# A recurrent-layer encoder step on one core: norm of two column blocks laid out half a weight tile earlier, two blocks of branch tile 4 ordered before the gates of tile 0

## The chip, the cores and the metric

The kernel runs on one core of a Trainium2 chip. The metric is device time in microseconds (us) of one execution. The engines of the core are named as in the profile: PE (TensorE matmul), PEld (its weight load), DVE (VectorE), ACT (ScalarE), POOL (GpSimd) and SP (SyncE, which here only issues DMAs). Each engine works through its own queue in order; semaphores order one engine's work behind another's.

## The reference, cut to what matters

The reference is one inference step of a two-layer encoder over 1024 new frames of one stream and 32 more frames of a second one (1056 tokens, model width 1024). Layer A is a gated linear recurrence of width 1408, layer B is attention in a sliding window. Only the first half of layer A is touched by the change:

```python
u = rmsnorm(x, norm_pre) @ w_in                 # 1024 -> 2 x 1408
branch, gate = u[..., :D_RNN], u[..., D_RNN:]
conv = conv_b + ext[:, 0:T] * conv_w[0]         # ext: branch behind 3 older rows
for tap in range(1, CONV_W):                    # 4 taps along time
    conv = conv + ext[:, tap:tap + T] * conv_w[tap]
xb = conv.reshape(B, T, 16, 88)                 # blocks of 88 channels
r = sigmoid(einsum('btnc,ncd->btnd', xb, w_r) + b_r)
i = sigmoid(einsum('btnc,ncd->btnd', xb, w_i) + b_i)
...
y = (h * silu(gate)) @ w_out
return x + rmsnorm(y, norm_post), new_conv, new_h
```

Each channel is convolved along time with four taps; the recurrence gates r and i are products of the convolved channels with 16 small matrices of 88 x 88.

## The kernel before, in words

**Layout.** Channels lie on the 128 partitions, tokens along the free dimension. The 1408 recurrent channels are 11 tiles of 128 (`MR`), the 1024 input channels 8 (`KD`). The tokens are three column blocks (`NSA`): 0 to 384, 384 to 768, and 768 to 1060 (292 columns, with three columns of gap). A product for one tile and one column block fills one bank of PSUM; `bank` hands out eight of them in turn.

**Precision.** A float32 product is made of three reduced ones: every operand is split into a high part and a residual (`split`, lines 112 to 117: ACT rounds, VectorE or POOL subtracts; names with `hi`/`h` and `lo`/`l`). `mm3` (lines 146 to 152) issues three matmuls for each of the contraction tiles, on lines 150, 151 and 152: 24 for one column block of a branch tile.

**The norm.** The RMS norm of a token is a factor for a column, and is applied after the product. `x_stat(n)` takes the squares of the rows of column block n on ACT (line 281), makes the reciprocal roots on VectorE (283 to 286) and writes them on diagonals (`diag`, 289). `x_norm(n)` (lines 291 to 306) spreads them over all partitions with three small matmuls against ones (line 296, tile `rs`, held in their order by `pin`), copies the result to SBUF on ACT (299 to 302), then evacuates that column block of the first three branch tiles with it (line 207, VectorE), and convolves them (line 222 on ACT for tap 0, line 224 on VectorE for taps 1 to 3) and splits the result into `chi` and `clo` (116, 117).

**The first three tiles** go by column block: all three tiles for block 0, then for block 1, then for block 2 (`first_mm`, lines 310 to 313, and the loop at 328 to 335). `x_norm(0)` stands behind the second tile of block 1, `x_norm(1)` behind the first tile of block 2, `x_norm(2)` behind the loop.

**Tiles 3 to 10** go whole (loop at 445 to 464). In step t the kernel traces the three blocks of branch tile t with their evacuation, the weights of tile t + 2 (`prep_in`), the convolution, the gate weights of tile t - 1, then the gates of the tile that `GATES_AT[t]` names (tile 0 in step 3), the split of the convolution and the packing of tile t - 1, and the recurrence.

**Gates.** A gate of tile t needs its own convolution (lines 150 to 152, in the profile `gt<-chi` and `gt<-clo`) and some rows of the neighbouring tiles, since 88 does not divide 128. These rows are gathered by DMA into a `pack` tile (`pack_rows`, line 371: high parts issued from ACT, residuals from SP), which two more matmuls use (390, 391). Tile 0 needs 48 rows of tile 1. Tile 0 has thirty gate matmuls: two gates, three column blocks, five each.

**Weights.** `weights` loads a tile of weights in two halves on SP's queue (line 129, ring `raw` of four), and splits them into rings of six. For the tiles in `LO_POOL` (here 3, 4, 5 and gates 0 and 1) POOL makes the residual.

**The order of each engine's queue** is made by a planner that runs over the traced program: it takes what is ready by its own estimates, in the order of the program, with parts under `urgent` ahead by 300 places. `pin` ties an instruction behind the one traced before it on the same engine.

Of the kernel before, what the change touches and what calls it, by code (L numbers as in the profile page):

```python
# [63 lines left out]
def _trunk(ctx, tc, nc, A):  # L64
# [11 lines left out]
    def urgent(offset=300):  # L76
        return tc.high_priority(offset=offset)

    def pin(i, on=True):
        return tc.keep_in_program_order(i) if on else i  # L80

    def bank(name, tag="mm", bufs=None):
        return psum.tile([P, 512], F32, tag=tag, name=name, bufs=bufs or nbank)
# [28 lines left out]
    def split(dst_hi, dst_lo, src, lo_eng=None, hi_dve=False, behind=False):  # L112
        if hi_dve:
            V.tensor_copy(dst_hi, src)
        else:
            pin(S.activation(dst_hi, src, AF.Copy), behind)  # L116
        (lo_eng or V).tensor_tensor(dst_lo, src, dst_hi.bitcast(F32), op=ALU.subtract)  # L117
# [5 lines left out]
    def weights(src, kn, name, gain=None):  # L123

        out = []
        for k0 in range(0, kn, 4):
            kk = min(4, kn - k0)
            raw = ring.tile([P, 4, P], F32, tag="raw", bufs=4, name=f"raw_{name}_{k0}")
            nc.sync.dma_start(raw[:, :kk, :], src[:, k0:k0 + kk, :])
            if gain is not None and name not in GAIN_ACT:  # L130
                with urgent():
                    G.tensor_tensor(raw[:, :kk, :], raw[:, :kk, :],
                                    gains[:, gain * KD + k0:gain * KD + k0 + kk].unsqueeze(2).to_broadcast([P, kk, P]),
                                    op=ALU.mult)
            hi = ring.tile([P, 4, P], F32R, tag="whi", bufs=6, name=f"whi_{name}_{k0}")
            lo = ring.tile([P, 4, P], F32R, tag="wlo", bufs=6, name=f"wlo_{name}_{k0}")
            with urgent():
                if name in GAIN_ACT:
                    for i in range(kk):
                        split_scaled(hi[:, i, :], lo[:, i, :], raw[:, i, :], g_of(gain, k0 + i))  # L140
                else:
                    split(hi[:, :kk, :], lo[:, :kk, :], raw[:, :kk, :], G if name in LO_POOL else None, name in HI_DVE)
            out += [(hi[:, i, :], lo[:, i, :]) for i in range(kk)]
        return out

    def mm3(ps, ws, xs, last=True):

        n = len(ws)
        for i, ((wh, wl), (xh, xl)) in enumerate(zip(ws, xs)):
            nc.tensor.matmul(ps, wh, xh, start=i == 0, stop=False)  # L150
            nc.tensor.matmul(ps, wh, xl, start=False, stop=False)  # L151
            nc.tensor.matmul(ps, wl, xh, start=False, stop=last and i == n - 1)  # L152

# [24 lines left out]
    def row(name, dt=F32, w=W + 3):  # L178
        return rows.tile([P, W + 3], dt, tag="row", bufs=NROW, name=name)[:, :w]

    wts = {}

    def prep_in(m):
        wts[m] = weights(A["w_in_a"][m], KD, f"ina{m}")

    def x_of(c0, c1):
        return [(xhi[k][:, c0:c1], xlo[k][:, c0:c1]) for k in range(KD)]

    conv, chl, ext, gw, pack = {}, {}, {}, {}, {}

    def branch_mm(t, ns=(0, 1, 2)):
        if t not in ext:
            ext[t] = row(f"ext{t}")
            G.memset(ext[t][:, 0:3], 0.0)
        banks = []
        for n in ns:
            c0, c1 = NSA[n]
            ps = bank(f"br{t}_{n}")
            mm3(ps[:, :c1 - c0], wts[t], x_of(c0, c1))
            banks.append((n, ps))  # L200
        return banks

    def branch_evac(t, banks):
        for n, ps in banks:
            c0, c1 = NSA[n]
            with urgent():
                V.tensor_tensor(ext[t][:, 3 + c0:3 + c1], ps[:, :c1 - c0], rs[:, c0:c1], op=ALU.mult)

    def branch_conv(t, n=None):

        c0, c1 = (0, W) if n is None else NSA[n]
        e = ext[t]
        if c0 == 0:
            conv[t] = row(f"conv{t}", w=W)
            chl[t] = (row(f"chi{t}", F32R, W), row(f"clo{t}", F32R, W))
        if c1 == W:
            G.tensor_copy(convst[:, t, 0, :], e[:, SEQ:SEQ + 3])
            G.tensor_copy(convst[:, t, 1, :], e[:, S0 + DEC:S0 + DEC + 3])
            G.tensor_copy(e[:, S0:S0 + 3], pa[:, t, 9:12])
            del ext[t]  # L220
        c = conv[t][:, c0:c1]
        pin(S.activation(c, e[:, c0:c1], AF.Identity, bias=pa[:, t, 4:5], scale=pa[:, t, 0:1]), n == 0)  # L222
        for k in (1, 2, 3):
            V.scalar_tensor_tensor(c, e[:, c0 + k:c1 + k], pa[:, t, k:k + 1], c, op0=ALU.mult, op1=ALU.add)  # L224
        if n is not None:
            split(*(x[:, c0:c1] for x in chl[t]), c)
# [48 lines left out]
    def x_stat(n, rows_):  # L275

        s, y, m, r = (stat[:, i, 3 * n:3 * n + 3] for i in range(4))
        with urgent():
            for t, xr in zip(range(3 * n, 3 * n + 3), rows_):
                k = P if t < 8 else DEC  # L280
                pin(S.activation(xr[:k], xr[:k], AF.Square, accum_out=stat[:k, 0, t:t + 1]), t in (0, 3))
            S.activation(y, s, AF.Abs_reciprocal_sqrt, bias=epst, scale=1.0 / 1024.0)
            V.tensor_scalar(m, s, 1.0 / 1024.0, EPS, op0=ALU.mult, op1=ALU.add)
            V.tensor_tensor(m, m, y, op=ALU.mult)
            V.scalar_tensor_tensor(m, m, -0.5, y, op0=ALU.mult, op1=ALU.mult)
            V.scalar_tensor_tensor(r, m, 1.5, y, op0=ALU.add, op1=ALU.mult)
            for i, t in enumerate(range(3 * n, 3 * n + 3)):
                k = P if t < 8 else DEC
                V.tensor_scalar(diag[:k, t * P:t * P + k], ident[:k, :k], stat[:k, 3, t:t + 1], None, op0=ALU.mult)

    def x_norm(n):

        ps = bank(f"rs{n}")
        for i, t in enumerate(range(3 * n, 3 * n + 3)):
            m = P if t < 8 else DEC
            pin(nc.tensor.matmul(ps[:, i * P:i * P + m], ones[:m], diag[:m, t * P:t * P + m], start=True, stop=True))
        with urgent():
            if n < 2:
                S.activation(rs[:, NSA[n][0]:NSA[n][1]], ps[:, :384], AF.Copy, scale=1024.0)
            else:  # L300
                S.activation(rs[:, 768:SEQ], ps[:, :256], AF.Copy, scale=1024.0)
                S.activation(rs[:, S0:S0 + DEC], ps[:, 256:256 + DEC], AF.Copy, scale=1024.0)
        for m in range(NS):
            branch_evac(m, open_[n][m])
        for m in range(NS):
            branch_conv(m, n)

    open_ = {0: [], 1: [], 2: []}

    def first_mm(n, m):  # L310
        if n == 0 and m:
            prep_in(m)
        open_[n].append(branch_mm(m, (n,)))

    x_split(0)
    for m in range(NS):
# [10 lines left out]
    x_stat(1, xr[1])  # L327
    for n in (1, 2):
        for m in range(NS):
            first_mm(n, m)  # L330
            if m == 2 - n:
                x_norm(n - 1)
        if n == 1:
            x_stat(2, xr[2])
    x_norm(2)
# [26 lines left out]
    def prep_gate(t):  # L362
        gw[t] = weights(A["wg"][t], 4 + 2 * (NATIVE[t] is not None), f"gate{t}")

    def pack_rows(t):

        pk = row(f"pack{t}", F32R, W)
        h, off = sum(n for _, _, n in PACKED[t]), 0
        for s_, r0, n in PACKED[t]:
            for x in range(2):  # L370
                (nc.sync if x else nc.scalar).dma_start(pk[x * h + off:x * h + off + n, :].bitcast(F32),
                                                       chl[s_][x][r0:r0 + n, :].bitcast(F32))
            off += n
        pack[t] = (pk, 2 * h)
# [69 lines left out]
    GATES_AT = ((), (), (), (0,), (1,), (2,), (3,), (4,), (5,), (6,), (7,), (8, 9, 10))  # L444
    for t in range(MR):
        if t >= NS:
            branch_evac(t, branch_mm(t))
        wts.pop(t)
        if t >= NS - 2:
            prep_in(t + 2)  # L450
        with urgent():
            if t >= NS:
                branch_conv(t)
            if t >= 1:
                prep_gate(t - 1)
        ri = [gates(i) for i in GATES_AT[t]]
        with urgent():
            if t >= NS:

                split(*chl[t], conv[t], behind=True)  # L460
            if t >= 1:
                pack_rows(t - 1)
        for i, g in zip(GATES_AT[t], ri):
            recur(i, g)
# [183 lines left out]
    for n in (1, 2):  # L648
        last = orders[-1][:-1 - REUSE:-1]
        orders.append(last + [m for m in orders[-1] if m not in last])  # L650
    na = []
    for n, order in enumerate(orders):
        zs, acc = {}, []
        w = NSB[n][1] - NSB[n][0]
        for i, m in enumerate(order):
            if i + 1 < KD and f"{n}_{order[i + 1]}" not in wts:
                prep_outa(n, order[i + 1])
            ws = wts[f"{n}_{m}"]
            if n < 2 and i >= KD - REUSE:
                wts[f"{n + 1}_{m}"] = ws  # L660
            ps = bank(f"oa{m}_{n}")[:, :w]
# [579 lines left out]
```

## Time and profile before

| | |
|---|---|
| median of three runs | 914.59 us (914.43 to 915.57) |
| the profiled execution | 918.22 us, its span 916.4 us |
| TensorE busy | 891.0 us, 97% of the span |
| VectorE busy | 721.5 us, 79% |
| ACT busy | 562.8 us, 61% |
| POOL busy | 212.5 us, 23% |
| mean granted TensorE clock | 0.993 |

Times in the profile count from the start of the span. In a timeline a row is: start, duration, engine, line, operation, output <- inputs, shapes, how many of them, and in brackets how long the engine had been idle before it and which instruction released it. A matmul's duration covers its passage through the array, so the step from one start to the next is the time that it costs. In the view of windows a row is a stretch: its length, then busy time and number of instructions of PE, PEld, DVE, ACT and POOL, the granted TensorE clock as a share of full speed, the share of the DMA engines that is busy, and GB/s. The list of waits gives for each pair the total, the number and the longest.

### The profile page before, as it was taken

What the parts mean: (1) busy time and instruction counts of PE and PEld (TensorE: products, weight loads), DVE (VectorE), ACT (ScalarE), POOL (GpSimd) and SP (SyncE); (2) the same over time, 40 slices, a digit from 0 to 9 for tenths busy, and PEclk for the clock granted to TensorE, in tenths of its full rate; (3) what the DMA queues carried; (4) which work ended last, traced back from release to release, by engine and by line L of the source; (5) the groups of instructions that cost most, each with busy time, mean ns of one, the idle gap of its engine ahead of it and who ended that gap; (6) DMA issues with size and microseconds to landing.
All of it is one profiled execution on the core that took longest, in us unless ns stands there. A gap on an engine that the chain in (4) does not pass through costs nothing.

```text
span 916.4 us, 15897 instructions
## 1 busy us (share of the span) xinstructions
PE 891.0 (97%) x5434; PEld 864.6 (94%) x5434; DVE 721.5 (79%) x1571; ACT 562.8 (61%) x1231; POOL 212.5 (23%) x263
## 2 busy tenths in 40 slices
PE   9989999999999999999999999999999999899997
PEld 8989999999999999999989899999999998889985
DVE  5796878878897663185987758999989998898686
ACT  8747877869453334364663327666666766797661
POOL 5240222114300001124354521122212111202130
PEclk9989999999999999999999999999999999999999
DMA  9532433342543325445556586256347346424884
GB/s 336 197 84 67 134 94 118 93 123 88 174 134 118 89 83 163 133 145 183 161 173 191 167 235 155 95 158 184 96 131 212 95 118 183 136 96 137 288 268 160
DMA packets 95778, 137.35 MB, mean 150 GB/s; under 512 B 16145, under 2 KB 64305, under 8 KB 95697
## 3 DMA queue, kind: packets, MB, share of 16 engines
q1 hardware_dynamic: 86040, 123.30, 44.4%
q10 hardware_dynamic: 9480, 12.49, 4.4%
q8 instruction: 43, 0.70, 0.3%
q0 software_dynamic: 176, 0.54, 0.2%
q14 instruction: 39, 0.31, 0.1%
HBM read 99.28 MB, written 32.13 MB: 143 GB/s over the span
## 4 chain that ended last, share of the span: by engine, by line
PE 62%; DVE 19%; DMA 4%; ACT 3%; issue 3%; SPq 1%; POOL 1%; DVEq 0%; ACTq 0%; POOLq 0%
PE gb L151 5%; PE gb L152 5%; PE gb L150 5%; PE obm L698 4%; PE gB L698 4%; PE oa L151 4%; PE oa L150 4%; PE oa L152 4%; PE br L151 3%; PE br L150 3%; PE br L152 3%; PE ot L698 2%; DVE T L967 2%; DVE pl L117 2%; DVE P L927 2%
## 5 line engine op out<-in xcount | busy, mean ns | idle before, releaser
L150 PE MATMUL oa<-yh,whi_outa 128*128 128x384 f32 (+1 forms) x264 | 85.8, 325 | 0.0
L151 PE MATMUL gb<-xlo,whi_ina 128*128 128x384 f32 (+1 forms) x264 | 85.5, 324 | 0.0
L152 PE MATMUL gb<-xhi,wlo_ina 128*128 128x384 f32 (+1 forms) x264 | 85.3, 323 | 0.0
L150 PE MATMUL gb<-xhi,whi_ina 128*128 128x384 f32 (+1 forms) x264 | 85.1, 322 | 0.0
L151 PE MATMUL oa<-yl,whi_outa 128*128 128x384 f32 (+1 forms) x264 | 85.1, 323 | 0.0
L152 PE MATMUL oa<-yh,wlo_outa 128*128 128x384 f32 (+1 forms) x264 | 85.0, 323 | 0.0
L930 ACT ACTIVATE P<-P,sm 128x256 f32<-128x256 f32 (+1 forms) x132 | 64.0, 486 | 26.4 <-DVE sm L927 26.1
L150 PE MATMUL br<-xhi,whi_ina 128*128 128x384 f32 (+1 forms) x240 | 78.4, 327 | 0.0
L151 PE MATMUL br<-xlo,whi_ina 128*128 128x384 f32 (+1 forms) x240 | 78.4, 326 | 0.0
L152 PE MATMUL br<-xhi,wlo_ina 128*128 128x384 f32 (+1 forms) x240 | 77.8, 325 | 0.0
L117 DVE TENSOR_TENSOR wlo_outa<-raw_outa,whi_outa 128x512 fp32r<-128x512 f32 (+1 forms) x60 | 43.7, 741 | 42.0 <-ACT whi_outa L116 41.9
L616 POOL TENSOR_TENSOR qp<-qp,qp 128x384 f32<-128x384 f32 (+2 forms) x34 | 39.2, 1154 | 149.4 <-ACT qp L614 137.5
L698 PE MATMUL gB<-xh,whi_g 128*128 128x384 f32 (+1 forms) x192 | 63.2, 329 | 0.0
L698 PE MATMUL gB<-xh,wlo_g 128*128 128x384 f32 (+1 forms) x192 | 63.1, 329 | 0.0
L698 PE MATMUL gB<-xl,whi_g 128*128 128x384 f32 (+1 forms) x192 | 62.9, 328 | 0.0
L116 ACT ACTIVATE whi_outa<-raw_outa 128x512 fp32r<-128x512 f32 (+1 forms) x60 | 35.4, 594 | 41.9 <-PE oa L151 24.3
L224 DVE SCALAR_TENSOR_TENSOR conv<-ext,pa,conv 128x1060 f32<-128x1060 f32 (+2 forms) x51 | 50.1, 1005 | 9.0 <-ACT conv L222 8.6
L927 DVE CUSTOM_DVE_ANT_0 P<-S,mask,nsnk 128x256 f32<-128x256 f32 (+1 forms) x128 | 52.8, 461 | 0.1
L150 PEld LDWEIGHTS oa<-yh,whi_outa 128*128 128x128 f32 x264 | 49.6, 188 | 0.4
L151 PEld LDWEIGHTS oa<-yl,whi_outa 128*128 128x128 f32 x264 | 49.5, 188 | 0.4
L152 PEld LDWEIGHTS oa<-yh,wlo_outa 128*128 128x128 f32 x264 | 49.6, 188 | 0.0
L150 PEld LDWEIGHTS gb<-xhi,whi_ina 128*128 128x128 f32 x264 | 49.6, 188 | 0.0
(303 smaller groups left out, 2913.2 us busy)
## 6 DMA issues: line engine op xcount, KB each, us to landing
raw_ina<-w_in_a SPq DMA_DIRECT2D x44, 256.0 KB, 2.9
raw_outa<-w_out_a SPq DMA_DIRECT2D x40, 256.0 KB, 2.6
raw_ob<-w_out_b SPq DMA_DIRECT2D x32, 256.0 KB, 2.7
qscr<-quadq SPq DMA_DIRECT2D x8, 768.0 KB
Q<-qscr SPq DMA_DIRECT2D x32, 192.0 KB, 5.2
hscr<-u SPq DMA_DIRECT2D x11, 530.0 KB, 3.3
xr<-xr SPq DMA_DIRECT2D x8, 512.0 KB, 10.3
raw_g<-w_in_b SPq DMA_DIRECT2D x16, 256.0 KB, 2.6
```

What stands on the lines that cost most here:

```text
L116: pin(S.activation(dst_hi, src, AF.Copy), behind)
L117: (lo_eng or V).tensor_tensor(dst_lo, src, dst_hi.bitcast(F32), op=ALU.subtract)
L150: nc.tensor.matmul(ps, wh, xh, start=i == 0, stop=False)
L151: nc.tensor.matmul(ps, wh, xl, start=False, stop=False)
L152: nc.tensor.matmul(ps, wl, xh, start=False, stop=last and i == n - 1)
L224: V.scalar_tensor_tensor(c, e[:, c0 + k:c1 + k], pa[:, t, k:k + 1], c, op0=ALU.mult, op1=ALU.add)
L616: G.tensor_tensor(sums[0], sums[0], q, op=ALU.add)
L698: nc.tensor.matmul(ps, l, r, start=c == 0, stop=c == 3 * n - 1)
L927: V.tensor_tensor_reduce(pt[:, h, :w], sb[:, (h - h0) * 256:(h - h0) * 256 + w], msk, -0.125, nsnk[:, sk][:, h:h + 1], op0=ALU.add, op1=AL ...
L930: S.activation(pt[:, h, :w], pt[:, h, :w], AF.Exp, bias=nmax[:, h:h + 1], scale=-1.0, accum_out=rsum[:, h:h + 1])
L967: V.tensor_tensor(TT[g, n][h // 2][64 * (h % 2):64 * (h % 2) + 64, c0:c0 + q], ob[:64, h * q:(h + 1) * q], half[:64, h * q:(h + 1) * q], o ...
```

## The change

Two edits.

The first passes `x_norm(n - 1)` into the product as `mid`: `mm3` calls it between the fourth and the fifth of its eight contraction tiles, so the three `rs` matmuls and all that follows from them are traced in the middle of the block and not behind it: norm 0 in the second tile of block 1, norm 1 in the first tile of block 2. The first matmul behind them is pinned to its place, and so is the first matmul of the next tile (`behind`).

The second traces column blocks 0 and 1 of branch tile 4, and their evacuation, in step 3: behind the weights of tile 5, ahead of the convolution of tile 3 and of the gates of tile 0. Step 4 then has only block 2 of that tile.

```diff
-    def mm3(ps, ws, xs, last=True):
+    def mm3(ps, ws, xs, last=True, mid=None, behind=False):
         n = len(ws)
         for i, ((wh, wl), (xh, xl)) in enumerate(zip(ws, xs)):
-            nc.tensor.matmul(ps, wh, xh, start=i == 0, stop=False)
+            if mid and i == n // 2:
+                mid()
+            pin(nc.tensor.matmul(ps, wh, xh, start=i == 0, stop=False), behind and i == 0 or mid and i == n // 2)
             nc.tensor.matmul(ps, wh, xl, start=False, stop=False)
             nc.tensor.matmul(ps, wl, xh, start=False, stop=last and i == n - 1)
...
     for n in (1, 2):
         for m in range(NS):
-            first_mm(n, m)
-            if m == 2 - n:
-                x_norm(n - 1)
+            first_mm(n, m, (lambda: x_norm(n - 1)) if m == 2 - n else None, m == 3 - n)
         if n == 1:
             x_stat(2, xr[2])
     x_norm(2)
...
     for t in range(MR):
         if t >= NS:
-            branch_evac(t, branch_mm(t))
+            branch_evac(t, branch_mm(t, (2,) if t == 4 else (0, 1, 2)))
         wts.pop(t)
         if t >= NS - 2:
             prep_in(t + 2)
+        if t == 3:
+            branch_evac(4, branch_mm(4, (0, 1)))
         with urgent():
             if t >= NS:
                 branch_conv(t)
```

`branch_mm` and `first_mm` hand the two new arguments on.

More of the change, by code (lines that the diff above doesn't have):

```diff
@@ L189, in _trunk, with branch_mm @@
     conv, chl, ext, gw, pack = {}, {}, {}, {}, {}
-    def branch_mm(t, ns=(0, 1, 2)):
+    def branch_mm(t, ns=(0, 1, 2), mid=None, behind=False):
         if t not in ext:
@@ L198, in branch_mm @@
             ps = bank(f"br{t}_{n}")
-            mm3(ps[:, :c1 - c0], wts[t], x_of(c0, c1))
+            mm3(ps[:, :c1 - c0], wts[t], x_of(c0, c1), mid=mid, behind=behind)
             banks.append((n, ps))
@@ L308, in _trunk, with first_mm @@
     open_ = {0: [], 1: [], 2: []}
-    def first_mm(n, m):
+    def first_mm(n, m, mid=None, behind=False):
         if n == 0 and m:
             prep_in(m)
-        open_[n].append(branch_mm(m, (n,)))
+        open_[n].append(branch_mm(m, (n,), mid, behind))
     x_split(0)
```

## The prediction

> **What bounds the kernel now.** I read the page first, for which engine fills the span and where the TensorE clock dips.
>
> ```profile
> span 916.4 us, 15897 instructions
> PE 891.0 (97%) x5434; PEld 864.6 (94%) x5434; DVE 721.5 (79%) x1571; ACT 562.8 (61%) x1231; POOL 212.5 (23%) x263
> PEclk9989999999999999999999999999999999999999
> ```
>
> TensorE is busy for 97% of the span, so time is won only where it waits or runs slowly. The third digit of the clock row is one such place (45.8 to 68.7 us). Next I read TensorE's list of waits over the whole span, whose longest entry names its cause, and then its timeline around that entry.
>
> ```profile
> PE gt L150 <- ACT chi L116: 3.6, 1, 3.6
> PE rAk L698 <- DVE wlo_kA L121: 1.9, 2, 1.6
> PE rAk L698 <- DVE xl L117: 1.3, 1, 1.3
> ```
>
> ```profile
> 49.62 0.34 PE L150 MATMUL br<-xhi,whi_ina 128*128 128x384 f32 x1
> ...
> 53.80 0.30 PE L150 MATMUL br<-xhi,whi_ina 128*128 128x292 f32 x1
> ...
> 57.02 0.33 PE L150 MATMUL gt<-chi,whi_gate 128*128 128x384 f32 x1
> ...
> 61.84 0.93 PE L150 MATMUL gt<-chi,whi_gate 128*128 128x292 f32 x2 [3.61 <-ACT chi L116]
> ...
> 68.16 0.34 PE L150 MATMUL br<-xhi,whi_ina 128*128 128x384 f32 x1
> ...
> 71.82 0.34 PE L390 MATMUL gt<-pack,whi_gate 96*128 96x384 f32 x1
> ...
> 80.13 0.34 PE L150 MATMUL gt<-chi,whi_gate 128*128 128x384 f32 x1
> ```
>
> The gates of tile 0 begin at 57.02, run six matmuls, and then stand 3.61 us for the third block of tile 0's split convolution (chi). The rest of those gates and all of branch tile 4 follow until 80.13, where the gates of tile 1 start. The windows view shows the second cost, the granted clock after the wait:
>
> ```profile
> 62.00:64.00 2.00, 2.00 (x7) 2.00 (x8) 2.00 (x6) 1.12 (x3) 1.57 (x1) 0.50 0.29 100
> 66.00:68.00 2.00, 2.00 (x8) 2.00 (x8) 1.10 (x1) 1.98 (x2) 0.00 (x0) 0.50 0.66 158
> 68.00:70.00 2.00, 2.00 (x13) 2.00 (x12) 1.93 (x3) 0.17 (x1) 0.00 (x0) 1.00 0.39 138
> ```
>
> The clock is 0.50 in both stretches before 68, with 7 and 8 matmuls in 2 us where 13 fit at full clock.
>
> **What the stretch could take at best.** Between 49.62 and 53.80 lie the 24 matmuls of one 384-wide block: 0.174 us each. Between 53.80 and 57.02 lie 24 of 292: 0.134 us each. From 57.02 to 80.13 the code asks for tile 4's three blocks (48 wide, 24 narrow) and tile 0's gates (20 wide, 10 narrow). That is 68 x 0.174 + 34 x 0.134 = 16.4 us of work in 23.1 us. So 6.7 us is there to win: the 3.6 us wait, and 3.1 us from the half clock (61.84 to 68.16 is 6.3 us, half of it lost).
>
> A sentence apart on this term: the Trainium skill (TensorE: Matmul & The Clock Gate, Part 1) says the clock follows a free-running window of about 3.4 us. By that rule another execution pays one or two windows at half clock, 1.7 to 3.4 us in place of 3.1, and the gain below would be 4.2 to 5.9. The trace cannot show the phase of other executions.
>
> **Part two of the change: blocks 0 and 1 of tile 4 ahead of the gates of tile 0.** Nothing is added: 48 matmuls, the memset of ext4 on POOL and two evacuations on VectorE move up; no DMA does. TensorE gets 48 x 0.174 = 8.4 us of work at 57.02, so it reaches the gates at 65.4. The chi that it waited for came at 61.84, so the whole wait is covered with 3.6 us to spare, and with it the half clock. Without that cover the wait and the clock's term come back. The weights of tile 4 are ready: tiles 3, gate 0, 4, gate 1 pass POOL's residual line in that order, and the last of tile 4 is there by 47.1.
>
> ```profile
> 45.73 1.32 POOL L117 TENSOR_TENSOR wlo_ina<-raw_ina,whi_ina 128x512 fp32r<-128x512 f32 x1 [0.25 <-ACT whi_ina L116]
> 62.56 1.20 DVE L117 TENSOR_TENSOR clo<-conv,chi 128x292 fp32r<-128x292 f32 x3
> 63.68 1.38 DVE L207 TENSOR_TENSOR ext<-br,rs 128x384 f32<-128x384 f32 x3
> ```
>
> PSUM has eight banks. Tile 3 holds three until VectorE evacuates them (63.68 to 65.06), tile 4 now holds two, so three of the gates' six banks are free at once; the fourth is asked for at 65.4 + 5 x 0.174 x 2 + 5 x 0.134 = 67.8 (two wide blocks and a narrow one, five matmuls each). The price is nothing; VectorE would have to be 2.7 us later than now before it cost anything.
>
> What is late next is the packed operand. Tile 0's gates need rows of tile 1's convolution, copied by DMA (L371) after tile 1's last residual.
>
> ```profile
> 64.00 0.55 SPq L371 DMA_DIRECT2D pack<-clo  x1
> pack<-clo SPq DMA_DIRECT2D x1, 198.8 KB, 5.3
> ```
>
> The 198.8 KB copy is tile 0's pack (48 rows), issued at 64.00 with 5.3 us to landing: 69.3. Now the pack matmul at 71.82 comes after it, because thirty matmuls of tile 4 stand between. After the change they have already run, and I take the gates in their written order: three matmuls on chi, then the pack. TensorE would want it at 65.4 + 3 x 0.174 = 65.9. With an unchanged landing this is a new wait of 3.4 us, with everything behind it on TensorE's queue (the other 25 gate matmuls, tile 4's third block, the gates of tile 1); if the pack matmuls are put later, it is 0. What decides is how much sooner VectorE finishes.
>
> **Part one: the laying out of norms 0 and 1 in the middle of a block.** Three small matmuls (rs) move up by half a block, the next matmul is pinned behind them, and with them one ACT copy, three evacuations, and the convolution steps of three tiles can start. Counts stay the same.
>
> ```profile
> 29.27 0.38 PE L296 MATMUL rs<-diag,ones 128*128 128x128 f32 x2
> 37.33 0.38 PE L296 MATMUL rs<-diag,ones 128*128 128x128 f32 x2
> 30.83 0.49 ACT L299 ACTIVATE rs<-rs 128x384 f32<-128x384 f32 x1 [1.26 <-PE rs L296]
> 25.36 0.67 DVE L289 TENSOR_SCALAR diag<-ident,stat 128x128 f32<-128x128 f32 x3
> 31.36 1.49 DVE L207 TENSOR_TENSOR ext<-br,rs 128x384 f32<-128x384 f32 x3 [1.58 <-ACT rs L299]
> 34.37 0.67 DVE L289 TENSOR_SCALAR diag<-ident,stat 128x128 f32<-128x128 f32 x3
> 36.64 1.17 DVE L284 TENSOR_TENSOR stat<-stat 128x3 f32<-128x3 f32 x1 [0.99 <-ACT stat L282]
> ```
>
> The matmuls of norm 0 go from 29.27 to 27.2, sooner by half a wide block (12 x 0.174 = 2.1 us); their diag is written by 26.0, so they do not wait. ACT is busy with squares until 29.57 (30.83 less its wait) and then stands 1.26 us for them, so its copy comes 1.26 us sooner, or up to 2.1 if it is ordered between two squares. VectorE stood 1.58 us for that copy and 0.99 us for ACT's statistics at 36.64; behind that it is nearly full until the last residual at 63.76. So the end of that work moves by 0 (the idle time only shifts to the second wait) to 1.58 + 0.99 = 2.6 us. I take 2.3: the copy's 1.26 and the second wait, since ACT reaches the statistics sooner too. Norm 1 moves from 37.33 to 34.12 + half of 3.21 = 35.7; its diag is written by 35.04 as it is, 0.7 us ahead: no cost. The row for 34.12:
>
> ```profile
> 34.12 0.30 PE L150 MATMUL br<-xhi,whi 128*128 128x292 f32 x1
> ```
>
> **The sum.** The pack lands at 69.3 - 2.3 = 67.0 against 65.9: a wait of 1.1 us (0.8 to 3.4 by the bounds, 0 if the order is another). Gain: 6.7 - 1.1 = 5.6 us. Everything from 80.13 to the end of layer A moves with TensorE: in 300 to 400 us it shows no idle time. Later stages start from what it delivers.
>
> ```profile
> 300.00:400.00 100.00, 100.00 (x595) 99.73 (x594) 47.51 (x95) 41.87 (x81) 8.67 (x9) 1.00 0.41 120
> 500.00:600.00 100.00, 96.82 (x624) 93.69 (x623) 77.15 (x210) 54.84 (x153) 31.79 (x33) 1.00 0.54 160
> 600.00:700.00 100.00, 97.92 (x639) 93.42 (x638) 92.87 (x293) 65.46 (x190) 23.05 (x22) 1.00 0.58 161
> ```
>
> The profiled execution took 918.22 us (916.4 of span, 1.8 around it), which would become 912.6. It stands 3.6 above the median of the runs, 914.59; the same gain from that gives 909.0. Whether the 1.1 us wait brings the half clock back is read from two rows: the wait of 1.3 us (rAk on xl) lies in 500 to 600 us, where the clock stays 1.00; the ones of 1.6 and 0.3 us (1.9 in two) were followed by this:
>
> ```profile
> 471.00:474.20 3.20, 3.20 (x10) 3.04 (x10) 3.20 (x13) 0.50 (x2) 0.00 (x0) 0.50 0.47 146
> ```
>
> So 1.1 us alone should be free of it, and 1.9 us or more may cost another 3.2 us at half speed, 1.6 us. The Trainium skill (TensorE: Matmul & The Clock Gate, Why this matters for your kernels) puts the limit at idle gaps of about 3 us; the trace disagrees with its 1.9. By the page a wait of 2 us would cost 2 us only, and the sum would be 4.7; by the row it would be 3.1.
>
> **Rivals.**
>
> *A long second wait.* VectorE's idle time only shifts, the pack lands at 69.3, TensorE stands 3.4 us at it and runs 3.2 us at half clock: 6.7 - 3.4 - 1.6 = 1.7 us, 912.9. For it: the pack's copies queue behind one another on SP and the landing is a third of a block away. Against it: the 1.26 us that ACT stood is plainly given up.
>
> *Given back.* The gates keep their place in TensorE's order, or later stages where VectorE decides take the 5.6 us: 914.6. For it: VectorE is busy 92.9 of 100 us in 600 to 700. Against: TensorE is busy 97.9 there, and VectorE's work waits for its products.
>
> *Slower: norm 1 asks for its diag too early.* Its rs matmuls stand in the middle of a block with 12 matmuls pinned behind them. If the statistics of rows 3 to 5 are ordered behind the convolution of block 0, which may now start sooner (nine steps of VectorE at 0.62 us: 5.6), diag 1 is written at 40.6 in place of 35.04. TensorE then stands 4.9 us and loses 3.1 to the clock, 8.0 against 5.6 won: 917.0. It decides once diag 1 comes after 38.2, where 2.5 + 3.1 = 5.6. Against it: VectorE now does these statistics between the convolution steps.
>
> ```profile
> 33.18 0.62 DVE L224 SCALAR_TENSOR_TENSOR conv<-ext,pa,conv 128x384 f32<-128x384 f32 x1
> ```
>
> **How the numbers follow.** Forecast 0.70, 909.0, its own range 907.9 (the full 6.7, pack on time) to 910.6 (a wait of 2.7 us with the clock untouched). Long second wait 0.13, given back 0.10, slower 0.07. The range 907.2 to 913.2 adds 0.7 below for the 1.1 us that the runs shown lie apart (914.43 to 915.57), reaches over the long wait above, and leaves out the last two cases and little else. What a measurement of this kernel can tell from no change is about 0.2%, 1.8 us: faster means below 912.8. The forecast and half of the long wait lie there, 0.77; same 0.16; slower 0.07.
>
> **What would show it.** Right: after tile 3's last block, 48 br matmuls and only then gt; no wait of 3.6 us on chi; clock 1.00 in 60 to 80 us; the gates of tile 1 beginning near 74.5 in place of 80.13; the last clo of the three tiles ending near 61.5; a wait of about 1 us at the first pack matmul (L390). Wrong: rs matmuls that wait for diag, a pack wait above 2 us with clock 0.50 behind it, or gates of tile 1 at 74.5 with an unchanged span.

## The result, and the profile after

The changed kernel takes 911.4 us (median of 12 runs, 908.26 to 914.2) beside 915.25 us of the kernel before on the same chip (median of 12, 914.37 to 918.73). The ratio of the runs is 0.995, with an interval of 0.9934 to 0.9966: 4.6 us are won (3.1 to 6.0). The two medians themselves lie 3.9 us apart. The profiled execution took 908.26 us, 906.5 of it span. That is 10 us below the profiled execution of before, so the two pages must not simply be subtracted. In the code every line of `mm3` and behind it stands two lines further down now (150 is 152, 296 is 298), and from the loop behind `first_mm` on the numbers are nearly as before.

TensorE is busy for 98% of the span. The clock row of the page of the changed kernel:

```profile
PEclk9999999999999999999999999999999999999999
```

The dip in the third slice of the clock row is gone. That row alone proves little: a second profile of the kernel before, taken further down, shows nines throughout as well, although 3.4 us at half clock lie in it. TensorE's waits over the whole span no longer hold the one on chi (line waited for, total, times, longest; us):

```profile
PE ot L700 <- ACT zb L1045: 1.8, 1, 1.8
PE rAk L700 <- DVE wlo_kA L121: 1.7, 2, 1.4
PE rs L298 <- DVE diag L291: 0.3, 1, 0.3
```

The first two lie after 400 us and have counterparts before. The third is new and belongs to the change. TensorE's timeline around the changed place:

```profile
34.02 0.30 PE L152 MATMUL br<-xhi,whi 128*128 128x292 f32 x1
...
45.60 0.41 PE L298 MATMUL rs<-diag,ones 32*128 32x32 f32 x2 [0.33 <-DVE diag L291]
...
54.06 0.30 PE L152 MATMUL br<-xhi,whi_ina 128*128 128x292 f32 x1
...
65.66 0.34 PE L152 MATMUL gt<-chi,whi_gate 128*128 128x384 f32 x1
...
66.18 0.34 PE L390 MATMUL gt<-pack,whi_gate 96*128 96x384 f32 x1
...
73.75 0.34 PE L152 MATMUL gt<-chi,whi_gate 128*128 128x384 f32 x1
```

Tile 3's third block begins at 54.06, tile 4's two blocks end at 65.66, and there the gates of tile 0 begin: three matmuls on chi, then the pack at 66.18, without a wait. The gates of tile 1 begin at 73.75. From tile 3's third block to there it is 73.75 - 54.06 = 19.69 us; before it was 80.13 - 53.80 = 26.33. The windows view shows full speed in it, here for the first of the gates:

```profile
66.00:68.00 2.00, 2.00 (x14) 2.00 (x14) 1.96 (x3) 0.97 (x2) 0.00 (x0) 1.00 0.00 1
```

So this stage gives 6.6 us. Its beginning costs a little: from the first 292-wide matmul (34.02) to tile 3's third block it is 20.04 us, and was 53.80 - 34.12 = 19.68 before. The loss of 0.36 us contains the new wait of 0.33 of `rs` on `diag`. Net, the change is worth 6.3 us in this pair of profiles.

How VectorE came to be early enough is read from ACT's and VectorE's timelines and from the issue and landing of the pack:

```profile
27.06 0.83 PE L298 MATMUL rs<-diag,ones 128*128 128x128 f32 x6
27.93 0.49 ACT L301 ACTIVATE rs<-rs 128x384 f32<-128x384 f32 x1 [0.20 <-PE rs L298]
28.45 1.49 DVE L209 TENSOR_TENSOR ext<-br,rs 128x384 f32<-128x384 f32 x3 [0.45 <-ACT rs L301]
58.37 1.21 DVE L117 TENSOR_TENSOR clo<-conv,chi 128x292 fp32r<-128x292 f32 x3
59.81 0.55 SPq L371 DMA_DIRECT2D pack<-clo  x1
pack<-clo SPq DMA_DIRECT2D x1, 198.8 KB, 4.8
```

The copy of `rs` begins at 27.93 in place of 30.83, the first evacuation at 28.45 in place of 31.36 (2.9 us sooner), the last residual of the three tiles at 58.37 in place of 62.56 (4.2 sooner), and the pack is issued at 59.81 and lands 4.8 us later, at 64.6.

### The profile page after: what moved, and what is told of

Read it like the earlier page. It is cut to its first block, busy times and chain, and to the rows that moved or that the text cites. A ratio compares the mean times of both kernels' runs of the same rounds, so it can differ in the third digit from the quotient of the medians.

```text
span 906.5 us, 15896 instructions
## 1 busy us (share of the span) xinstructions
PE 886.4 (98%) x5434; PEld 861.9 (95%) x5434; DVE 715.6 (79%) x1571; ACT 563.7 (62%) x1231; POOL 211.1 (23%) x263
## 4 chain that ended last, share of the span: by engine, by line
PE 77%; DVE 12%; DMA 5%; ACT 3%; issue 2%; SPq 1%; DVEq 0%; ACTq 0%
PE gB L700 6%; PE gb L153 5%; PE gb L154 5%; PE gb L152 5%; PE oa L153 5%; PE oa L152 5%; PE br L153 5%; PE oa L154 4%; PE br L152 4%; PE br L154 4%; PE obm L700 4%; PE rAq L700 3%; PE rBq L700 3%; PE ot L700 3%; PE T L951 2%; PE O L961 2%
## 5 line engine op out<-in xcount | busy, mean ns | idle before, releaser
L117 DVE TENSOR_TENSOR wlo_outa<-raw_outa,whi_outa 128x512 fp32r<-128x512 f32 (+1 forms) x60 | 45.9, 776 | 41.8 <-ACT whi_outa L116 41.6
L618 POOL TENSOR_TENSOR qp<-qp,qp 128x384 f32<-128x384 f32 (+2 forms) x34 | 43.0, 1264 | 146.3 <-ACT qp L616 120.6
L226 DVE SCALAR_TENSOR_TENSOR conv<-ext,pa,conv 128x1060 f32<-128x1060 f32 (+2 forms) x51 | 46.2, 927 | 10.7 <-ACT conv L224 10.2
```

What stands on the lines that cost most here:

```text
L618: G.tensor_tensor(sums[0], sums[0], q, op=ALU.add)
```

## The experiments

Six kernels take the change apart, and each of the two kernels was profiled once more, to see what differs from one execution to the next. All diffs are against the changed kernel. The ratios are to the kernel before on the same chip.

**The blocks of tile 4 alone**, the norms laid out as before:

```diff
-            first_mm(n, m, (lambda: x_norm(n - 1)) if m == 2 - n else None, m == 3 - n)
+            first_mm(n, m)
+            if m == 2 - n:
+                x_norm(n - 1)
```

> The two blocks of tile 4 ahead of tile 0's gates, the norms laid out where they were before. My theory (VectorE's earlier end is what brings the packed rows in time): VectorE ends the first three tiles near 63.7 us as before, the pack lands near 69, TensorE wants it near 66, so it waits 2 to 3.5 us at the first pack matmul, with or without a half-clock window behind it; of the 6.4 us by which the gates of tile 1 begin sooner in the changed kernel 1.5 to 4.5 remain; time ratio to before 0.995 to 0.998. Rival (the norm's place is worth nothing, the blocks do it all): no wait at the pack above 0.5 us, gates of tile 1 at 73.5 to 74.5 us, the same ratio as the changed kernel, 0.995 or below.

It took 915.56 us, ratio 1.0003 (0.9989 to 1.0018): nothing is won, where the expectation left a part of the gain. From the timelines of VectorE and TensorE, and a window of the slow stretch:

```profile
63.68 1.20 DVE L117 TENSOR_TENSOR clo<-conv,chi 128x292 fp32r<-128x292 f32 x3
70.47 0.66 PE L392 MATMUL gt<-pack,whi_gate 96*128 96x384 f32 x1 [3.31 <-DMA pack<-clo]
80.98 0.34 PE L152 MATMUL gt<-chi,whi_gate 128*128 128x384 f32 x1
72.00:74.00 2.00, 2.00 (x9) 2.00 (x8) 0.40 (x1) 0.65 (x2) 0.00 (x0) 0.50 0.00 0
```

The wait on chi is gone and stands again, 3.31 us of it, one operand later, at the pack, and from shortly before its end the clock is at half for 6.8 us. This is the rival of the long second wait, which was put at 3.4 us of wait and 1.6 us for the clock; the wait had the right size, the clock cost 3.4. The stage takes 26.09 us (its third block begins at 54.89), against 26.33 in the kernel before. The blocks do cover the wait on chi, but as long as the pack comes no sooner, that only shifts it.

**The norms alone**, tile 4 behind the gates as before:

```diff
-            branch_evac(t, branch_mm(t, (2,) if t == 4 else (0, 1, 2)))
+            branch_evac(t, branch_mm(t))
...
-        if t == 3:
-            branch_evac(4, branch_mm(4, (0, 1)))
```

> The norms in the middle of a block, tile 4 left behind the gates of tile 0. Theory (the wait is lateness of VectorE's work, and the earlier norm takes 4.2 us off it, more than the 3.6 us wait): chi of the third block is there near 58.1, when TensorE has just done the six gate matmuls before it; wait on chi under 0.5 us, clock 1.00 in 60 to 80 us, gates of tile 1 at 74 to 75 us, ratio within 0.001 of the changed kernel's 0.995. Rival (the norm's place only shifts idle time, the blocks are needed): a wait on chi of 1.5 us or more stays and gates of tile 1 begin after 76; ratio 0.997 to 1.0.

911.53 us, ratio 0.9953 (0.9935 to 0.9971): as good as the whole change by the timed runs. From its timeline and windows:

```profile
64.88 0.45 PE L390 MATMUL gt<-pack,whi_gate 96*128 96x384 f32 x1 [0.84 <-DMA pack<-clo]
75.70 0.34 PE L152 MATMUL gt<-chi,whi_gate 128*128 128x384 f32 x1
66.00:68.00 2.00, 2.00 (x14) 2.00 (x14) 1.67 (x2) 2.00 (x6) 0.00 (x0) 1.00 0.08 31
```

With the norms sooner, chi is in time without any cover. The pack comes 0.84 us late, the clock stays at 1.00 behind that wait. The stage takes 21.23 us (its third block begins at 54.47) beside 19.69 of the whole change. Beside early norms the blocks are thus worth at most 1.5 us there, which the runs cannot tell.

**One block, and three, of tile 4 in front of the gates**, the norms as in the change:

```diff
-            branch_evac(t, branch_mm(t, (2,) if t == 4 else (0, 1, 2)))
+            branch_evac(t, branch_mm(t, (1, 2) if t == 4 else (0, 1, 2)))
...
-            branch_evac(4, branch_mm(4, (0, 1)))
+            branch_evac(4, branch_mm(4, (0,)))
```

```diff
-            branch_evac(t, branch_mm(t, (2,) if t == 4 else (0, 1, 2)))
+            branch_evac(t, branch_mm(t, () if t == 4 else (0, 1, 2)))
...
-            branch_evac(4, branch_mm(4, (0, 1)))
+            branch_evac(4, branch_mm(4, (0, 1, 2)))
```

> Norms in the middle, one block of tile 4 (4.2 us) ahead of the gates and not two. Theory: TensorE reaches the gates near 61.5; chi is there (58.1 to 59); the pack, which lands near 64.5 in the changed kernel, is wanted after nine matmuls near 63.0, so a wait of 1 to 2 us at the pack and gates of tile 1 at 75 to 76; ratio 0.995 to 0.998. Rival (anything that covers the chi wait is enough): no wait, gates of tile 1 near 73.8, the ratio of the changed kernel.

> Norms in the middle, all three blocks of tile 4 ahead of the gates of tile 0. Theory: TensorE has no gap either way and the gates have more slack; gates of tile 1 begin near 73.8 as in the changed kernel and the ratio is the same within 0.001. Rival (tile 0's gates 3.2 us later make its recurrence, the banks or the gate weights late): a new wait above 0.5 us before 100 us, ratio 0.997 or more.

One block: 912.38 us, ratio 0.9965 (0.9943 to 0.9987). Three blocks: 912.4 us, 0.9969 (0.9952 to 0.9986). Both intervals overlap with that of the changed kernel (0.9934 to 0.9966), so the timed runs do not tell one, two and three blocks apart; what follows is from the profiles. With three blocks the stage takes 19.69 us as with two and TensorE's only wait between 20 and 110 us is the 0.3 us on `diag`. With one block it takes 23.07 us, in an execution 3 us slower than the median; the list and a window show:

```profile
PE gt L390 <- DMA pack<-clo: 1.6, 1, 1.6
68.00:70.00 2.00, 2.00 (x8) 2.00 (x8) 1.35 (x2) 1.13 (x3) 0.00 (x0) 0.50 0.00 0
```

Here 1.6 us of wait was enough to bring the half clock, in this execution for 3.4 us. So one block is not always enough, and a third adds nothing to the stage. In these profiles the place where the pack stops being late lies between one block and two.

**One norm at a time**, the blocks as in the change; `n == 1` lays out norm 0 in the middle of the block, and `n == 2` in its place norm 1:

```diff
-            first_mm(n, m, (lambda: x_norm(n - 1)) if m == 2 - n else None, m == 3 - n)
+            early = n == 1
+            first_mm(n, m, (lambda: x_norm(n - 1)) if early and m == 2 - n else None, early and m == 3 - n)
+            if not early and m == 2 - n:
+                x_norm(n - 1)
```

> The changed kernel, but only norm 0 moves to the middle of its block; norm 1 stands behind its block as before. Theory (the start of VectorE's work at the first evacuation, 2.9 us sooner, carries most of the shift): first evacuation near 28.5 us, last residual of the first three tiles by 61.5, the pack there before or at most 0.7 us after TensorE wants it; gates of tile 1 20 us after tile 3's third block starts, as in the changed kernel (19.7), ratio 0.994 to 0.997. Rival (each norm carries its own part): last residual after 62, a pack wait of 1 us or more, the gates 21 to 23 us after that block.

> The changed kernel, but only norm 1 moves; norm 0 stands behind its block as before. Theory: the first evacuation stays near 31.4 us, VectorE is full from there on, the last residual ends at 62.5 to 64 as before, the pack lands near 68 to 69 and TensorE waits 2 to 3.5 us for it, often with a half-clock window behind: gates of tile 1 22 to 26 us after tile 3's third block starts, ratio 0.997 to 1.001. Rival: last residual by 61.5 and the changed kernel's ratio.

Norm 0 alone: 910.65 us (9 runs), ratio 0.9945 (0.9926 to 0.9964). TensorE has no wait at all between 20 and 110 us. Its timeline:

```profile
33.59 0.30 PE L152 MATMUL br<-xhi,whi 128*128 128x292 f32 x1
...
53.28 0.30 PE L152 MATMUL br<-xhi,whi_ina 128*128 128x292 f32 x1
...
72.98 0.34 PE L152 MATMUL gt<-chi,whi_gate 128*128 128x384 f32 x1
```

From the first 292-wide matmul to tile 3's third block it is 53.28 - 33.59 = 19.69 us, without the loss of 0.36, and the stage takes 72.98 - 53.28 = 19.70. It is the lowest median of all, though its interval does not part it from the changed kernel.

Norm 1 alone: 918.97 us (10 runs), ratio 1.0033 (1.0009 to 1.0058), slower than before. Its VectorE row, its pack matmul, its longest wait and a late window:

```profile
61.91 1.19 DVE L117 TENSOR_TENSOR clo<-conv,chi 128x292 fp32r<-128x292 f32 x3
67.62 0.45 PE L393 MATMUL gt<-pack,whi_gate 96*128 96x384 f32 x1 [1.45 <-DMA pack<-clo]
PE rAq L703 <- DVE vc L770: 4.1, 1, 4.1
522.00:525.00 3.00, 3.00 (x11) 3.00 (x11) 0.00 (x0) 0.00 (x0) 0.00 (x0) 0.50 0.97 281
```

The stage itself is better than before, 21.41 us with 1.45 of wait, less than the 2 to 3.5 us expected. The loss lies 450 us further on, in the attention layer: 4.1 us of wait and half the clock over 6.8 us, 7.5 us together. The same matmul waits in the other nine profiles too, but only 0.3 to 1.0 us, and for another result of VectorE. First the kernel before, then this one:

```profile
PE rAq L698 <- DVE v L117: 0.3, 1, 0.3
525.91 0.81 DVE L765 TENSOR_TENSOR vc<-vc,r 128x288 f32<-128x288 f32 x2
```

```profile
519.47 0.81 DVE L770 TENSOR_TENSOR vc<-vc,r 128x288 f32<-128x288 f32 x2
```

VectorE is not late. Counted from TensorE's first `vc` matmul of this block (515.70 in the kernel before, 509.24 here), its `vc` rows begin after 10.21 us there and 10.23 here. TensorE's order there is the same in both. But before, `rAq` waited for `v`, which VectorE begins at 522.16, and with norm 1 alone it waits for `vc`, 3.7 us further down VectorE's queue. Why it does is not shown; that the product was given another PSUM bank, one that `vc` still held, would fit. That this wait, seen in one profile, is what lengthens the timed runs is likely and not shown.

Measured from the first 292-wide matmul, the last residual of the three tiles begins after 62.56 - 34.12 = 28.4 us in the kernel before and after 58.37 - 34.02 = 24.4 in the changed one. Of that gain of 4.1 us norm 0 alone gives 3.2 and norm 1 alone 0.5, counted to the end of that group of residuals (26.43 and 29.14 us in place of 29.64); the remaining 0.4 us appears only with both.

**The two kernels again, one execution each on the same chip:**

> The kernel before, once more with a trace. What is open: the stage up to the gates of tile 1 gave 6.6 us between the two profiles, the runs only 4.6 (3.1 to 6.0). Theory (the length of the wait and of the half-clock stretch differ from execution to execution): the time from the start of tile 3's third block to the gates of tile 1 is 23.5 to 26.5 us (26.3 in the profile shown). Rival (given back in later stages): 26.0 to 26.6 again, and the difference lies behind 200 us.

> The changed kernel once more with a trace. By both accounts the stage from tile 3's third block to the gates of tile 1 is 19.7 us again, with no gap; the theory has the rest of the span (from the gate branch's first matmul to the end) the same as in the kernel before within 2 us, 720 to 725; the rival has it 1.5 us or more above the one of the kernel before.

914.94 us before and 912.23 after. The rows of the kernel before, from its timeline, its list of waits and its windows:

```profile
53.20 0.30 PE L150 MATMUL br<-xhi,whi_ina 128*128 128x292 f32 x1
78.76 0.34 PE L150 MATMUL gt<-chi,whi_gate 128*128 128x384 f32 x1
PE gt L150 <- ACT chi L116: 3.6, 1, 3.6
PE gt L150 <- DVE ext L207: 0.4, 1, 0.4
62.00:64.00 2.00, 1.64 (x7) 1.19 (x7) 2.00 (x6) 0.52 (x2) 2.00 (x1) 0.62 0.32 69
66.00:68.00 2.00, 2.00 (x14) 2.00 (x13) 1.66 (x2) 1.55 (x2) 0.00 (x0) 1.00 0.68 201
```

The wait is the same 3.6 us, a second one of 0.4 us on an evacuation by VectorE is new, the clock is back at 66 and not at 68, and the stage takes 25.56 us, within the expectation and below the rival's 26.0 to 26.6. So the wait on chi stands in both executions of the old kernel, while the half clock costs one stretch of 3.4 us or two. The changed kernel's stage was 19.70 us again: 5.9 us won here, 6.6 in the first pair.

How much of that reaches the end is seen at the first matmul of the product for layer A's other half, the gate (gb), in the order before, before again, after, after again:

```profile
192.37 0.34 PE L150 MATMUL gb<-xhi,whi_ina 128*128 128x384 f32 x1
```

```profile
191.00 0.34 PE L150 MATMUL gb<-xhi,whi_ina 128*128 128x384 f32 x1
```

```profile
186.01 0.34 PE L152 MATMUL gb<-xhi,whi_ina 128*128 128x384 f32 x1
```

```profile
185.79 0.34 PE L152 MATMUL gb<-xhi,whi_ina 128*128 128x384 f32 x1
```

The gain is there nearly in full, 6.4 and 5.2 us. From this matmul to the end of the span it is 724.1 and 722.2 us before, 720.5 and 724.6 after: the rest of the program, the same in both kernels, differs by 4 us between two executions of the changed kernel. The expectation, the same within 2 us, is missed in both pairs: 3.6 us less after the change in the first, 2.4 more in the second. That decides nothing about its rival. A spread of that size goes with an interval 3 us wide over 12 runs.

## Why the prediction was right, and where it was not

The forecast of 909.0 us was made against 914.59, a gain of 5.6; measured were 4.6 (3.1 to 6.0). The time, 911.4, lies in the range of 907.2 to 913.2, 0.8 us above the forecast's own range, which ended at 910.6. The 2.4 us between forecast and median are made of 0.7, by which the runs of before lie higher here than the three shown, and of 1.7, by which the distance of the medians (3.9) is smaller than the 5.6. That the forecast of 5.6 lies so near the timed gain is in part luck: with two terms put as the first pair of profiles measured them (no wait at the pack, 0.36 us lost at the beginning of the stage) the sum would be 6.3.

**Right: what bounds it, and what there is to win.** 6.7 us were read from the stage; 6.6 went, and it now takes 19.69 us, 0.1 above what its matmuls alone were worked out to need. The 3.1 us of half clock in it are those of one execution; the second one paid for one stretch and not two.

**Right: the order, and that the pack is late next.** Tile 4's 48 matmuls, then the gates in their written order, three on chi and then the pack: TensorE was forecast there at 65.9 and came at 66.18. A wait of 3.4 us was forecast for the old landing; the kernel with the blocks alone shows 3.31.

**Too simple: at which wait the clock falls.** The prediction read a bound from two rows (1.3 us free, 1.9 us in two waits followed by half clock). The rows are read rightly, and between 20 and 900 us no wait of 1.27 us or less was followed by half clock in any profile, so 1.1 us by itself would have been free of it. But above that the length of a wait gives no bound: waits of 1.45 and 1.86 us left the clock at 1.00, others of 1.3 to 1.6 did not. What does decide is in the last section. None of this came into the sum in the end, since no such wait was left in the stage.

**Wrong in size: how much sooner VectorE is done.** The prediction took 2.3 us of at most 2.6; it was 4.2. The step that failed first is the copy on ACT, "1.26 us sooner, or up to 2.1": it came 2.9 sooner. The three `rs` products, two matmuls each in the trace, had been counted as one event at 29.27. The kernel before ran two of the six there and the other four only at 30.19, between matmuls of the block, so ACT waited for those:

```profile
29.27 0.38 PE L296 MATMUL rs<-diag,ones 128*128 128x128 f32 x2
30.19 0.60 PE L296 MATMUL rs<-diag,ones 128*128 128x128 f32 x4
```

In the changed kernel the six stand in one row at 27.06, held together by the pin behind them, and ACT's copy sits between two squares. The other term, VectorE's second wait, was not won: between the first evacuation and the last residual (31.36 to 62.56 before, 28.45 to 58.37 after) VectorE stood 1.5 us before and 2.8 after. In its place its own work there became shorter, 27.2 us and not 29.7. One place is seen in the rows: four steps of the convolution, begun at 43.71, took 4.28 us in the kernel before, while POOL worked on three residuals, and eight took 4.31 in the changed kernel, while POOL stood at one (45.47 and 45.48 in the fence of the next paragraph). The prediction had no term for this. So the pack landed at 64.6, ahead of the 66.18 at which it is asked for, and the wait of 1.1 us in the sum was 0.

**Wrong: "Norm 1 ... no cost".** It costs 0.36 us, and not at its own place: its own `rs` did not wait. VectorE had more of the convolution to do by then, wrote the diagonals of norm 2 later, and met POOL's residuals there. The diagonals of norm 2 in the kernel before, then VectorE's and POOL's timeline of the changed kernel:

```profile
39.67 0.62 DVE L289 TENSOR_SCALAR diag<-ident,stat 128x128 f32<-128x128 f32 x3
```

```profile
41.60 1.42 POOL L117 TENSOR_TENSOR wlo_gate<-raw_gate,whi_gate 128x512 fp32r<-128x512 f32 x1 [1.41 <-ACT whi_gate L116]
41.80 3.75 DVE L291 TENSOR_SCALAR diag<-ident,stat 128x128 f32<-128x128 f32 x3
42.99 2.52 POOL L117 TENSOR_TENSOR wlo_ina<-raw_ina,whi_ina 128x512 fp32r<-128x512 f32 x2
45.47 4.31 DVE L226 SCALAR_TENSOR_TENSOR conv<-ext,pa,conv 128x384 f32<-128x384 f32 x8
45.48 5.93 POOL L117 TENSOR_TENSOR wlo_gate<-raw_gate,whi_gate 128x512 fp32r<-128x512 f32 x1
```

The three diagonals take 3.75 us here, and 0.62 in the kernel before, where POOL had no residual between 39.61 and 40.50. In part it is the slower rival's mechanism, a diagonal ordered behind the convolution, with norm 2 in the place of norm 1 and at a twentieth of its price; POOL had no part in that rival. With norm 0 alone both the wait and the 0.36 us are gone.

**Right by the sum, wrong by its parts: what each half of the change is worth.** The prediction let the moved blocks cover the wait on chi and gave the norms the part of shortening the next one. The runs show the reverse weight. The blocks alone win nothing, the norms alone win what the whole wins. Both waits, chi and pack, hang on the same work of VectorE. To bring it 4 us forward removes the first and all but 0.84 us of the second, while 8.4 us of work put in front only takes away the first.

**Smaller than the stage: the timed gain.** Of 5.5 to 6.3 us net in the two pairs of profiles the timing shows 4.6, and its interval holds the 5.5. Part of the difference may be the one stretch of half clock or two. An estimate of the clock's share: averaged over the timed runs, one less the granted clock, times the span, is 7.8 us (35 runs on one chip) and 7.1 us (18 on another) for the kernel before and 4.7 us (12 runs) for the changed one. By it some 2.4 to 3.1 us of the gain are clock, and the rest is time in which TensorE no longer stands. It is a rough one: for the kernel with the blocks alone the figure is 5.9 us, and that kernel won nothing. Whether something of the 5.5 is given back behind 186 us is not settled, since that part varies by 4 us from execution to execution.

## What to carry to other kernels

When a wait is to be covered with other work, look for what else hangs on the same late producer: if the next operand comes from it too, the cover only moves the wait by one instruction, and the producer must be brought forward. To find what the producer waits for, read the chain back to its first late step and look whether several small instructions that together release it are run as one group or scattered between others; here six small matmuls pinned together in the middle of a block gave more than their shift of half a block. A part of a change that is priced at nothing deserves a run without it: with norm 1 left at its place nothing was lost and a wait was gone.

## What the runs showed of the hardware that was not expected

**The same wait is followed by half the clock in one execution and not in the next.** In every profile the moments at which the clock changes lie whole multiples of 3.413 us apart. In the kernel before, for example, the slow stretches of this stage and of the attention layer begin at 61.19 and 470.79, 120 such pieces from each other. The changed kernel and its second execution both wait 1.39 us at the same matmul of the attention layer. Here are that wait and the two pieces around it, first in the one, then in the other:

```profile
461.93 0.45 PE L700 MATMUL rAk<-xh,wlo_kA 128*128 128x384 f32 x1 [1.39 <-DVE wlo_kA L121]
460.14:463.56 3.42, 1.73 (x9) 1.04 (x7) 3.42 (x4) 3.33 (x12) 3.26 (x4) 1.00 0.19 70
463.56:466.97 3.41, 3.41 (x12) 3.09 (x11) 3.41 (x12) 0.75 (x3) 0.86 (x2) 0.50 0.26 87
```

```profile
461.73 0.44 PE L700 MATMUL rAk<-xh,wlo_kA 128*128 128x384 f32 x1 [1.39 <-DVE wlo_kA L121]
458.05:461.46 3.41, 2.29 (x17) 1.98 (x15) 3.41 (x4) 3.38 (x12) 3.33 (x3) 1.00 0.59 201
461.46:464.87 3.41, 2.74 (x11) 1.80 (x12) 3.41 (x6) 2.46 (x9) 2.68 (x4) 1.00 0.01 2
```

In the first the wait lies within one piece, TensorE stands 1.69 us of it, and the next piece runs at half. In the second a border cuts the wait in two, TensorE stands 1.12 and 0.67 us, and the clock stays at 1.00. Counted over the ten profiles, from 20 to 900 us of the span: a piece at full clock in which TensorE stood up to 1.30 us was never followed by half clock, of twelve with 1.32 to 1.45 us one was, and all fifteen with 1.47 us or more were. These are all 16 slow stretches. The length of the wait by itself does not tell: of 28 waits of 1.31 to 1.56 us twelve have half clock behind them, and two of 1.84 and 1.86 us have not. This is also why the same 3.6 us cost one piece or two: in the kernel before a border fell into the wait, 0.65 us ahead of its end, so that the next piece was slow and began with a gap as well; in its second execution the border came 1.25 us behind the end. The rule is read from the profiles, and no run moved a wait against the borders on purpose.

The slow stretches have one length or twice that, which fits the free-running window of about 3.4 us of the Trainium skill (TensorE: Matmul & The Clock Gate, Part 1). The limit of about 3 us for an idle gap that the Trainium skill gives (TensorE: Matmul & The Clock Gate, Why this matters for your kernels) did not hold for those twelve waits of 1.3 to 1.6 us.

**VectorE and POOL hold each other up.** In the fence on norm 2 a diagonal takes about 1.3 us, as long as a residual on POOL, and took about 0.2 us in the kernel before (three in 0.62). Once VectorE goes on to eight steps of the convolution without a pause, POOL's residual takes 5.93 us in place of 1.4. The Trainium skill (SBUF — State Buffer, SBUF: two separate sides) describes a pair of ports that the two engines lock for a whole instruction; the rows agree with it. Which of the two goes next, one instruction in turn as with the diagonals or eight in a row as with the convolution, they do not explain.
